# A decoder block on one core: all transposes of x put ahead of the modulation's rows, the rotary and lambda preparation moved into the first group, and the first weights loaded in four pieces

## The chip, the core and the metric

The kernel runs on one core of a Trainium2 chip. The metric is the device time of one execution in microseconds (us). A core has a matrix engine (TensorE, PE in the profile; its weight loads are PEld), a vector engine (VectorE, DVE), an activation engine (ScalarE, ACT), a general engine (GpSimd, POOL) and a queue engine that issues most transfers (SyncE, SP). Each engine takes its instructions in program order and waits for semaphores of the others.

## What is computed

One hybrid decoder block on x of 512 tokens by 1024 channels, float32. What matters here is its beginning:

```python
mod = (c @ w_ada[l] + b_ada[l])[:, None, :]
shift1, scale1, gate1, shift2, scale2, gate2 = jnp.split(mod, 6, axis=-1)
h = rmsnorm(x, norm1_w[l]) * (1.0 + scale1) + shift1
proj = h @ w_in[l]
...
qk = jax.nn.silu(causal_conv(jnp.concatenate([q_m, k_m], axis=-1), conv_w[l], conv_b[l]))
...
qd = partial_rope(rmsnorm(qd, q_norm_w[l]), positions)
kd = partial_rope(rmsnorm(kd, k_norm_w[l]), positions)
...
lam = (jnp.exp(jnp.sum(lam_q1[l] * lam_k1[l])) - jnp.exp(jnp.sum(lam_q2[l] * lam_k2[l])) + lam_init).astype(x.dtype)
```

After it come an mLSTM branch, a differential attention branch, an output projection and a mixture of 32 experts. The rotary tables (cos and sin of position times eight frequencies) and lambda are used only in the attention branch, long after the first projection.

## The kernel before, in words

The order of the instructions on each engine is the order in which the program text issues them; nothing reorders them later. Waits come from the tiles that instructions share and from the rings of buffers.

**Head.** SP loads x in four tiles of 128 tokens (L117), four lambda vectors of 64 numbers (L119), then through `load_ada0(fb)` (L142) the modulation weights of feature block fb, each block four transfers of 512 KB, with the first weights of `w_in` between them (`P0a`, units `wp`: one of 1024 KB and one loaded as two halves, L154 to L160). On POOL's own queue go the positions (L106) and, as broadcasts to all 128 partitions, the first 16 numbers of the q and k norm weights (`qkw16`, L109). SP waits at a transfer until the one eight places earlier has landed.

For each tile of x, ACT squares it and sums (L222), POOL makes the inverse root (L223, L193), DVE scales the tile (L225). `xT(j)` (L306) then transposes feature block j of all four tiles on PE (four transposes into one PSUM bank) and copies it back: even j on ACT (L315), odd j on DVE (L313). The banks are the four of ring `acc`, or for j of 4 and 5 the two of ring `t`.

`mod_rows(fb)` (L278) multiplies c with the modulation weights (16 matmuls on PE, L283) and ACT copies the row (L286); `mod_cols(fb)` (L288) turns the row into columns (8 small matmuls, L292) and DVE adds biases (L294 to L297) to the scale and shift `AB1`. `hT_pair(fb)` (L317) applies them to two blocks of x: the rounded part `hTh` on ACT (L324), the rest `hTl` on DVE (L325, L327). `warm(n)` issues n matmuls whose result nobody reads.

Between these calls of the head stand the angles (DVE L355 to L366, ACT Sin L368), lambda's products and Exp (L372 to L374, L384, L385), the rotary tables (eight DVE products, L382) and lambda's broadcast to the partitions (PE L394, DVE L395).

**First group.** `pstream` (L424) runs the projections as groups of eight chunks (a chunk is 128 rows of the contraction). `split` (L403) makes of a chunk's weights a rounded part `hi` on ACT (L407) and a rest `lo`, on POOL for one chunk and on DVE for the next (L408); it runs three chunks ahead. A chunk of the first group is 12 matmuls into four `acc` banks (L457 to L459). After chunk k, `hT_next(k)` (L329) adds the gate matmuls (L531, L532) and for k of 0, 2, 4 the next `mod_rows`, `mod_cols` and `hT_pair`. At a group's last chunk ACT copies out the four banks (L508, `craw`), and the next group's first chunk writes the same four banks. The convolutions of `ev_conv` (ACT L513, DVE L517, ACT Silu L524) follow through a list `later`; after each chunk `run` (L478) takes up to two of its entries, fewer when one answers "long". `param_cols` (L248: a small PE transpose and DVE steps L251 to L257) goes onto that list at k = 5 and so runs after chunk 5.

Of the kernel before, what the change touches and what calls it, by code (L numbers as in the profile page):

```python
# [33 lines left out]
R0, R1 = 3, 0  # L34
RT = (0, 0, 0, 0, 0)
REF = {4: 5, 7: 3, 11: 4}
W0 = (0, 2, 6)
EY, SY = 2, 0
W1 = 6
GF = False  # L40
# [17 lines left out]
def block_kernel(ctx, tc, x, c, positions, w_ada, b_ada, norm1_w, w_in, b_igate, b_fgate, conv_w, conv_b,  # L58
# [46 lines left out]
    mrow = dc.tile([24, 128], F32, name="mrow")  # L105
    G.dma_start(posi, positions[0].rearrange("(t p) -> t p", p=128))  # L106
    qkw16 = dc.tile([128, 2, 16], F32, name="qkw16")
    for i, w in enumerate((q_norm_w, k_norm_w)):
        G.dma_start(qkw16[:, i], bass.AP(tensor=w.tensor, offset=w.offset, ap=[[0, 128], [1, 16]]))  # L109
    cz = amc.rearrange("p a (k f) -> p (a k) f", f=32)  # L110
    S.dma_start(crow[0:8], c[0].rearrange("(j p) -> j p", p=128))
    S.dma_start(crow[8:16], norm1_w[0].rearrange("(j p) -> j p", p=128))
# [2 lines left out]
    xu = [U(f"x{a}", [128, 2, 1024]) for a in range(2)]  # L115
    for t in range(4):
        SP.dma_start(xu[t // 2][:, t % 2], x2[t * 128:(t + 1) * 128])  # L117
    for i, w in enumerate((lam_q1, lam_k1, lam_q2, lam_k2)):
        SP.dma_start(lamt[:, i], w)  # L119

    def ada_panel(ch, j):
        t = U("wada", [128, 2048])
# [19 lines left out]
    def load_ada0(fb):  # L142
        us = []
        for h in range(2):
            t = U("ada0", [128, 4, 2, 256])
            for s_ in range(2):
                SP.dma_start(t[:, :, s_], wada[h * 512:(h + 1) * 512, s_ * 1024 + fb * 256:s_ * 1024 + fb * 256 + 256]
                             .rearrange("(k p) f -> p k f", p=128))
            us.append(t)
        ada0[fb] = us  # L150

    P0a, P0b = [], []
    load_ada0(0)
    load_unit(P0a, 0, 0, 512)  # L154
    SP.dma_start(wif_raw, win[:, 2048:2056].rearrange("(k p) f -> p k f", p=128))
    load_ada0(1)
    P0a.append(U("wp", [128, 4, 512]))
    for i in range(2):
        SP.dma_start(P0a[1][:, 2 * i:2 * i + 2], win[512 + i * 256:768 + i * 256, 0:512].rearrange("(k p) f -> p k f", p=128))
        load_ada0(i + 2)  # L160
    SP.dma_start(rows[0:32], conv_w[0].rearrange("w (j p) -> (w j) p", p=128))
    SP.dma_start(rows[32:40], conv_b[0].rearrange("(j p) -> j p", p=128))
    SP.dma_start(rows[40:44], mlstm_norm_w[0])
# [165 lines left out]
    def hT_next(k):  # L329

        if GF:
            gates(k)
        if k in (0, 2, 4):
            fb = k // 2 + 1
            mod_rows(fb)
            if not GF:
                gates(k)
            mod_cols(fb)
            hT_pair(fb)
        elif not GF:  # L340
# [13 lines left out]
    for i in range(8):
        V.memset(invf[:, i:i + 1], INV_FREQ[i])  # L355
    xT(0)
    xT(1)
    V.tensor_mul(ang[:, 1], post[:, :, None].to_broadcast([128, 4, 8]), invf[:, None, :].to_broadcast([128, 4, 8]))
    V.tensor_scalar(kf, ang[:, 1], 1.0 / (2 * math.pi), MAGIC, op0=ALU.mult, op1=ALU.add)
    V.tensor_scalar(kf, kf, -MAGIC, None, op0=ALU.add)  # L360
    for cst in TWO_PI_PARTS:
        V.scalar_tensor_tensor(ang[:, 1], kf, -cst, ang[:, 1], op0=ALU.mult, op1=ALU.add)
    V.tensor_scalar(ang[:, 0], ang[:, 1], math.pi / 2, None, op0=ALU.add)
    V.tensor_scalar(kf, ang[:, 0], math.pi, -2 * math.pi, op0=ALU.is_gt, op1=ALU.mult)
    V.tensor_add(ang[:, 0], ang[:, 0], kf)
    V.tensor_scalar(ang, ang, -PI, PI, op0=ALU.max, op1=ALU.min)  # L366
    xT(2)
    S.activation(ang, ang, AF.Sin)  # L368
    xT(3)

    ls = dc.tile([1, 4], F32, name="ls")
    V.tensor_mul(lp, lamt[:, 0:4:2], lamt[:, 1:4:2])  # L372
    V.reduce_sum(ls[:, 0:2], lp, axis=AX.X)
    S.activation(ls[:, 0:2], ls[:, 0:2], AF.Exp)  # L374
    xT(4)
    xT(5)
    rope = []
    for i in range(2):
        tb = dc.tile([128, 4, 4, 8], F32, name=f"ropet{i}")

        for n, (cs, o_) in enumerate(((0, 0), (1, 8), (0, 8), (1, 0))):
            V.tensor_mul(tb[:, n], ang[:, cs], qkw16[:, i, None, o_:o_ + 8].to_broadcast([128, 4, 8]))  # L382
        rope.append(tb)
    V.tensor_sub(ls[:, 2:3], ls[:, 1:2], ls[:, 0:1])  # L384
    V.tensor_scalar(ls[:, 3:4], ls[:, 2:3], -(0.8 - 0.6 * math.exp(-0.3 * 0)), None, op0=ALU.add)  # L385
    warm(W0[0])
    mod_rows(0)
    xT(6)
    xT(7)
    warm(W0[1])  # L390
    mod_cols(0)
    nlam = const.tile([128, 1], F32, name="nlam")
    lamp = acc("lamp")
    PE.matmul(lamp[:, 0:1], ones[0:1, 0:1].to_broadcast([1, 128]), ls[:, 3:4], start=True, stop=True)  # L394
    V.tensor_copy(nlam, lamp[:, 0:1])  # L395
# [1133 lines left out]
```

## Time and profile before

| what | value |
|---|---|
| median of 3 runs | 716.75 us (714.95 to 717.03) |
| the profiled execution | 714.36 us, of which the span of instructions is 712.6 us |
| mean granted TensorE clock | 0.992 of full |
| PE busy | 669.8 us, 94% of the span |
| PEld, DVE, ACT, POOL busy | 69%, 53%, 33%, 28% |
| moved by DMA | 171.50 MB, mean 241 GB/s |

The rest, 1.76 us of the profiled execution, lies around the span. Times in the rows are us from the start of the span; where the rows merge several instructions, the count is behind "x" and the time is from the first one's start to the last one's end. The bracket at a row's end is the engine's idle time before it and what ended that.

### The profile page before, as it was taken

The page shows a single profiled execution, that of the slowest core. Times are in us where ns is not written, and L with a number is a line of the kernel's source. Part 1 is how long each engine was busy: PE and PEld are TensorE (multiplying, and loading weights), DVE is VectorE, ACT ScalarE, POOL GpSimd, SP SyncE. Part 2 cuts the span into 40 slices and gives each one's busy share as a digit, 9 for nine tenths or more (in the row PEclk, how much of TensorE's full clock was granted, in tenths as well). Part 3 has the DMA queues.
Part 4 walks back from the last instruction along what each step waited for, and adds up shares of the span by engine and source line. Part 5 has one row for each costly group of instructions (what it writes and reads, how often), then busy time and mean ns, then how long its engine had stood idle before and what let it go on. Part 6 is the DMA issues. An engine that isn't in the chain of part 4 may idle for free. (4 is left out here: it accounts for less than half of the span.)

```text
span 712.6 us, 11438 instructions
## 1 busy us (share of the span) xinstructions
PE 669.8 (94%) x4464; PEld 493.6 (69%) x4464; DVE 380.1 (53%) x765; ACT 236.1 (33%) x511; POOL 196.3 (28%) x204
## 2 busy tenths in 40 slices
PE   3999999999998999999999999699999999999972
PEld 2668887878777777778867888676667566766630
DVE  4746469866685467763795855763222332233211
ACT  5536582452443455542322234541111111111100
POOL 5213252436552213243253531121111121111100
PEclk9999999999999999999999999999999999999997
DMA  9973069215125011056636984779999999999971
GB/s 300 368 258 150 1 247 402 98 45 187 57 74 178 1 59 60 1 206 221 240 115 237 423 373 178 295 295 357 371 374 379 408 404 378 395 373 401 404 290 21
DMA packets 47386, 171.50 MB, mean 241 GB/s; under 512 B 8009, under 2 KB 16338, under 8 KB 32990
## 3 DMA queue, kind: packets, MB, share of 16 engines
q1 hardware_dynamic: 44510, 165.41, 60.2%
q0 software_dynamic: 2752, 5.28, 3.8%
q8 instruction: 37, 0.61, 0.3%
q14 instruction: 23, 0.19, 0.1%
q10 hardware_dynamic: 64, 0.02, 0.0%
HBM read 164.37 MB, written 10.51 MB: 245 GB/s over the span
## 5 line engine op out<-in xcount | busy, mean ns | idle before, releaser
L408 POOL TENSOR_TENSOR hl<-wp,hl 128x512 fp32r<-128x512 f32 x60 | 85.5, 1426 | 177.0 <-ACT hl L407 160.3
L407 ACT ACTIVATE hl<-wp 128x512 fp32r<-128x512 f32 x120 | 74.3, 627 | 104.0 <-PE acc L458 52.0
L1462 PE MATMUL gu<-we,he 128*64 128x256 f32 x784 | 93.2, 379 | 0.7 <-DMA we<-in_w_gate 0.7
L457 PE MATMUL acc<-hTh,hl 128*128 128x512 f32 x224 | 91.6, 409 | 0.3 <-ACT hTh L324 0.3
L458 PE MATMUL acc<-hTl,hl 128*128 128x512 f32 x224 | 88.4, 395 | 0.2 <-DVE hTl L327 0.2
L459 PE MATMUL acc<-hTh,hl 128*128 128x512 f32 x224 | 88.5, 395 | 0.0
L1462 PEld LDWEIGHTS gu<-we,he 128*64 128x64 f32 x784 | 59.6, 137 | 34.0 <-issue 6.8
L408 DVE TENSOR_TENSOR hl<-wp,hl 128x512 fp32r<-128x512 f32 x60 | 57.7, 963 | 46.8 <-ACT hl L407 46.8
L1308 PE MATMUL gp<-oh,xn 128*128 128x128 f16 x1024 | 64.0, 222 | 2.6 <-DVE oh L1296 1.7
L1308 PEld LDWEIGHTS <-xn 128*128 128x128 f16 x1024 | 60.2, 99 | 8.5 <-issue 5.4
L1469 ACT ACTIVATE sg<-gu 128x256 f32<-128x256 f32 x16 | 6.1, 383 | 173.5 <-PE gu L1462 173.5
L1493 POOL DMA_INDIRECT out<-y,ids x11 | 19.3, 1757 | 141.1 <-DVE y L1488 113.4
L1470 DVE TENSOR_TENSOR sg<-sg,gu 128x256 f32<-128x256 f32 x16 | 6.7, 421 | 94.4 <-ACT sg L1469 94.4
L457 PEld LDWEIGHTS acc<-hTh,hl 128*128 128x128 f32 x224 | 42.1, 188 | 15.4 <-issue 4.7
L461 PE MATMUL acc<-hl,hTh 128*128 128x512 f32 x128 | 52.5, 410 | 0.0
L463 PE MATMUL acc<-hl,hTl 128*128 128x512 f32 x128 | 50.2, 392 | 0.0
L462 PE MATMUL acc<-hl,hTh 128*128 128x512 f32 x128 | 50.1, 392 | 0.0
L1486 PE MATMUL o<-we,sg 128*64 128x512 f32 x192 | 48.3, 598 | 1.1 <-issue 1.1
L459 PEld LDWEIGHTS acc<-hTh,hl 128*128 128x128 f32 x224 | 42.2, 188 | 10.0
L458 PEld LDWEIGHTS acc<-hTl,hl 128*128 128x128 f32 x224 | 42.2, 188 | 9.1 <-DVE hTl L327 0.5
L826 DVE SCALAR_TENSOR_TENSOR wada<-wada,ccols 128x1024 f32<-128x1024 f32 x28 | 40.9, 1485 | 0.6 <-DMA wada<-in_w_ada 0.5
L1326 DVE TENSOR_SCALAR he<-gp,AB 128x128 f32<-128x128 f32 x64 | 21.9, 403 | 20.5 <-PE gp L1308 18.4
(353 smaller groups left out, 1148.9 us busy)
## 6 DMA issues: line engine op xcount, KB each, us to landing
we<-in_w_gate SPq DMA_DIRECT2D x25, 1024.0 KB
we<-in_w_up SPq DMA_DIRECT2D x24, 1024.0 KB
we<-in_w_down SPq DMA_DIRECT2D x24, 1024.0 KB
wp<-in_w_in SPq DMA_DIRECT2D x21, 1024.0 KB
wada<-in_w_ada SPq DMA_DIRECT2D x16, 1024.0 KB
ada<-in_w_ada SPq DMA_DIRECT2D x16, 512.0 KB
wx<-in_w_gate SPq DMA_DIRECT2D x6, 1024.0 KB
wp<-in_w_out SPq DMA_DIRECT2D x4, 1024.0 KB
```

The lines of the kernel that those rows point to most:

```text
L407: S.activation(hi, src, AF.Copy)
L408: (G if LP(n) else V).tensor_sub(lo, src, hi.bitcast(F32))
L457: PE.matmul(g.banks[b], wh[:, sl], ah, start=st, stop=False)
L458: PE.matmul(g.banks[b], wh[:, sl], al, start=False, stop=False)
L459: PE.matmul(g.banks[b], wl[:, sl], ah, start=False, stop=en)
L461: PE.matmul(g.banks[b], ah[:, sl], wh, start=st, stop=False)
L462: PE.matmul(g.banks[b], ah[:, sl], wl, start=False, stop=False)
L463: PE.matmul(g.banks[b], al[:, sl], wh, start=False, stop=en)
L826: V.scalar_tensor_tensor(t0[:, sl], cur[:, sl], ccol[:, j:j + 1], t0[:, sl], op0=ALU.mult, op1=ALU.add)
L1308: PE.matmul(ps_[c_][:, jj * 128:(jj + 1) * 128], part[t // 2][:, t % 2, c_ * 4 + jj], oh[i if st.get("first") else 2][:, t], start=first a ...
L1462: PE.matmul(gu[r, k * 256:(k + 1) * 256], h[:, j, r], wt[key, e][:, j], start=(j == 0), stop=(j == 7), skip_group_check=True)
L1486: PE.matmul(o[r], aT[:, j, r], wt["d", e][:, j, n * 512:(n + 1) * 512], start=(j == 0), stop=(j == 1), skip_group_check=True)
```

## The change

Four things are moved; the computation is the same.

1. All eight `xT(j)` stand ahead of `mod_rows(0)`; before, six did, and two stood behind it. `warm` is called with 0, 0 and 4 where it was 0, 2 and 6.
2. The frequencies, angles, Sin, lambda's products, Exp, rotary tables and lambda's broadcast become four functions `f0` to `f3`, put onto `later` behind `param_cols`: `param_cols` and `f0` run after chunk 5, `f1` and `f2` after chunk 6, `f3` and the first convolution after chunk 7. The broadcast's result sits in ring `t` instead of `acc`.
3. The two `qkw16` broadcasts are issued on POOL inside `f0`; the four lambda vectors are loaded by SP behind the row parameters of the first stage.
4. The first weights come as four pieces of 512 KB, each behind one block of modulation weights: block 0, piece 0, block 1, piece 1 and so on.

```diff
-W0 = (0, 2, 6)
+W0 = (0, 0, 4)
...
-    for i, w in enumerate((q_norm_w, k_norm_w)):
-        G.dma_start(qkw16[:, i], bass.AP(tensor=w.tensor, offset=w.offset, ap=[[0, 128], [1, 16]]))
...
-    for i, w in enumerate((lam_q1, lam_k1, lam_q2, lam_k2)):
-        SP.dma_start(lamt[:, i], w)
...
     load_ada0(0)
-    load_unit(P0a, 0, 0, 512)
-    SP.dma_start(wif_raw, win[:, 2048:2056].rearrange("(k p) f -> p k f", p=128))
-    load_ada0(1)
-    P0a.append(U("wp", [128, 4, 512]))
-    for i in range(2):
-        SP.dma_start(P0a[1][:, 2 * i:2 * i + 2], win[512 + i * 256:768 + i * 256, 0:512].rearrange("(k p) f -> p k f", p=128))
-        load_ada0(i + 2)
+    for i in range(4):
+        if i % 2 == 0:
+            P0a.append(U("wp", [128, 4, 512]))
+        SP.dma_start(P0a[i // 2][:, i % 2 * 2:i % 2 * 2 + 2],
+                     win[i * 256:i * 256 + 256, 0:512].rearrange("(k p) f -> p k f", p=128))
+        if i == 0:
+            SP.dma_start(wif_raw, win[:, 2048:2056].rearrange("(k p) f -> p k f", p=128))
+        if i < 3:
+            load_ada0(i + 1)
...
         elif k == 5:
             later.append(param_cols)
+            later.extend(angles())
...
+    def angles():
+        def f0():
+            for i, w in enumerate((q_norm_w, k_norm_w)):
+                G.dma_start(qkw16[:, i], bass.AP(tensor=w.tensor, offset=w.offset, ap=[[0, 128], [1, 16]]))
+            for i in range(8):
+                V.memset(invf[:, i:i + 1], INV_FREQ[i])
...
+        def f1():
...
+            V.tensor_scalar(ang, ang, -PI, PI, op0=ALU.max, op1=ALU.min)
+            S.activation(ang, ang, AF.Sin)
+            V.tensor_mul(lp, lamt[:, 0:4:2], lamt[:, 1:4:2])
+            V.reduce_sum(ls[:, 0:2], lp, axis=AX.X)
+            S.activation(ls[:, 0:2], ls[:, 0:2], AF.Exp)
+        def f2():
+            V.tensor_sub(ls[:, 2:3], ls[:, 1:2], ls[:, 0:1])
...
+        def f3():
...
+                    V.tensor_mul(tb[:, n], ang[:, cs], qkw16[:, i, None, o_:o_ + 8].to_broadcast([128, 4, 8]))
...
+            lamp = pt("lamp")
+            PE.matmul(lamp[:, 0:1], ones[0:1, 0:1].to_broadcast([1, 128]), ls[:, 3:4], start=True, stop=True)
+            V.tensor_copy(nlam, lamp[:, 0:1])
+        return [f0, f1, f2, f3]
+    for j in range(6):
+        xT(j)
     warm(W0[0])
+    for j in (6, 7):
+        xT(j)
     mod_rows(0)
-    xT(6)
-    xT(7)
     warm(W0[1])
     mod_cols(0)
```

On PE, between the transposes of blocks 4 and 5 and the first chunk, the order before was this (xtp are transposes, modp the modulation, lamp lambda's broadcast; two tiles of x, two transposes each, make a block):

```order
L283 MATMUL modp<-ada_99,amc 32x512 x4
L283 MATMUL modp<-ada_102,amc 32x512 x4
L309 MATMUL xtp<-ident,x_89 128x128 x2
L309 MATMUL xtp<-ident,x_90 128x128 x2
L309 MATMUL xtp<-ident,x_89 128x128 x2
L309 MATMUL xtp<-ident,x_90 128x128 x2
L276 MATMUL warm<-wi 64x512 x2
L292 MATMUL modp<-ones,ada_298 128x1 x4
L394 MATMUL lamp<-ls,ones 128x1
L276 MATMUL warm<-wi 64x512 x6
L457 MATMUL acc<-hTh_205,hl 128x512
```

and of the changed program at the same place:

```order
L311 MATMUL xtp<-ident,x_87 128x128 x2
L311 MATMUL xtp<-ident,x_88 128x128 x2
L285 MATMUL modp<-ada_93,amc 32x512 x4
L285 MATMUL modp<-ada_96,amc 32x512 x4
L294 MATMUL modp<-ones,ada_278 128x1 x4
L278 MATMUL warm<-wi 64x512 x4
L470 MATMUL acc<-hTh_204,hl 128x512
```

The last eight transposes went ahead of the modulation's rows; two of the warm matmuls in front of its columns, two behind them, and lambda's broadcast are gone from here.

On ACT, from the splits of chunks 8 and 9 (hl) on to the first group's copies (craw), the order before was this:

```order
L324 ACTIVATE hTh_206<-x_89,AB_204 128x256
L324 ACTIVATE hTh_206<-x_90,AB_204 128x256
L407 ACTIVATE hl<-wp 128x512 x3
L508 ACTIVATE craw<-acc 128x512 x4
L513 ACTIVATE cy<-craw,cols 128x512
```

and of the changed program:

```order
L420 ACTIVATE hl<-wp 128x512 x2
L379 ACT_TABLE_LOAD
L379 ACTIVATE ang<-ang 128x64
L383 ACT_TABLE_LOAD
L383 ACTIVATE ls<-ls 1x2
L420 ACTIVATE hl<-wp 128x512
L521 ACTIVATE craw<-acc 128x512 x4
```

Sin, Exp and a table load for each now stand between the split of chunk 9 and that of chunk 10, ahead of the four copies.

On DVE, behind `param_cols`, the changed program has the angles (f0, the split's lo of chunk 9, then f1), where before lo of chunk 9 came at once:

```order
L259 TENSOR_SCALAR qkcol<-qkcol 128x1
L366 MEMSET invf 128x1 x8
L367 TENSOR_TENSOR ang<-post,invf 128x32
L369 TENSOR_SCALAR kf<-ang 128x32
L370 TENSOR_SCALAR kf<-kf 128x32
L372 SCALAR_TENSOR_TENSOR ang<-kf,ang 128x32 x3
L421 TENSOR_TENSOR hl<-wp,hl 128x512
L375 TENSOR_SCALAR ang<-ang 128x32
L376 TENSOR_SCALAR kf<-ang 128x32
L377 TENSOR_TENSOR ang<-ang,kf 128x32
L378 TENSOR_SCALAR ang<-ang 128x64
```

All of these but the first and the split stood in the head before. Line numbers of the changed program are its own.

## Rows read from the trace of the kernel before

**Rows 1.** Whom PE waited for between 24 and 200 us: us in total, times, longest.
```profile
PE qkp L686 <- DVE E L615: 1.2, 2, 0.9
PE amp L568 <- DVE am L562: 0.6, 1, 0.6
PE acc L458 <- DVE hTl L327: 0.2, 1, 0.2
```

**Rows 2.** Timeline of PE in the head: start, us, instruction.
```profile
12.72 3.92 PE L309 MATMUL xtp<-ident,x 128*128 128x128 f32 x21 [1.48 <-DVE x L225]
16.58 1.92 PE L283 MATMUL modp<-ada,amc 128*32 128x512 f32 x16
...
20.32 0.95 PE L292 MATMUL modp<-ones,ada 128*128 128x1 f32 x8
...
23.42 0.51 PE L457 MATMUL acc<-hTh,hl 128*128 128x512 f32 x1 [0.32 <-ACT hTh L324]
```

**Rows 3.** Timeline of ACT in the head.
```profile
9.82 1.06 ACT L222 ACTIVATE junk<-x 128x1024 bf16<-128x1024 f32 x1 [1.41 <-DMA x<-in_x]
...
16.97 0.26 ACT L368 ACTIVATE ang<-ang 128x64 f32<-128x64 f32 x1
17.25 1.28 ACT L374 ACT_TABLE_LOAD   x1
18.54 0.20 ACT L374 ACTIVATE ls<-ls 1x2 f32<-1x2 f32 x1
...
19.18 0.57 ACT L286 ACTIVATE ada<-modp 128x512 f32<-128x512 f32 x1
...
22.27 2.08 ACT L324 ACTIVATE hTh<-x,AB 128x256 fp32r<-128x256 f32 x4 [1.48 <-DVE AB L297]
```

**Rows 4.** Timeline of DVE in the head.
```profile
9.96 0.75 DVE L225 TENSOR_SCALAR x<-x,ssq 128x1024 f32<-128x1024 f32 x1 [0.71 <-POOL ssq L193]
11.91 0.76 DVE L225 TENSOR_SCALAR x<-x,ssq 128x1024 f32<-128x1024 f32 x1 [1.20 <-POOL ssq L193]
...
14.76 0.18 DVE L358 TENSOR_TENSOR ang<-post,invf 128x32 f32<-128x32 f32 x1
...
16.74 0.20 DVE L366 TENSOR_SCALAR ang<-ang 128x64 f32<-128x64 f32 x1
...
21.57 0.60 DVE L297 TENSOR_TENSOR AB<-AB,ccols 128x2 f32<-128x2 f32 x1
```

**Rows 5.** One of the two broadcasts in the list of transfers (KB, and at the end us from issue to landing), and SP's issue of the first block of modulation weights, from the timeline.
```profile
qkw<-in_q_norm_w POOLq DMA_DIRECT2D x1, 8.0 KB, 6.8
...
6.17 4.00 SPq L147 DMA_DIRECT2D ada<-in_w_ada  x4
```

**Rows 6.** A stretch of 1 us: busy time of PE, PEld, DVE, ACT and POOL, then granted clock, DMA share and GB/s.
```profile
7.00:8.00 1.00, 0.19 (x2) 0.06 (x1) 0.81 (x4) 0.89 (x3) 0.68 (x2) 1.00 0.74 204
```

**Rows 7.** Stretches of 8 us, columns as in Rows 6.
```profile
0.00:8.00 8.00, 0.39 (x2) 0.29 (x2) 1.15 (x8) 4.33 (x6) 5.91 (x18) 1.00 0.78 244
8.00:16.00 8.00, 4.70 (x20) 3.83 (x21) 4.54 (x20) 3.25 (x9) 3.45 (x10) 1.00 1.04 351
16.00:24.00 8.00, 7.33 (x49) 4.13 (x47) 6.48 (x30) 6.42 (x14) 1.28 (x1) 1.00 1.10 357
24.00:32.00 8.00, 7.81 (x44) 4.90 (x45) 5.05 (x13) 3.60 (x9) 1.78 (x1) 1.00 1.08 372
```

**Rows 8.** Timeline of POOL: steps on x in the head, then lo of chunk 0 and of chunk 8.
```profile
8.54 0.75 POOL L223 TENSOR_SCALAR ssq<-ssq 128x1 f32<-128x1 f32 x1
9.38 0.55 POOL L193 TENSOR_TENSOR ssq<-ssq,mhalf 128x1 f32<-128x1 f32 x1
11.05 0.19 POOL L223 TENSOR_SCALAR ssq<-ssq 128x1 f32<-128x1 f32 x1 [1.13 <-ACT junk L222]
...
20.88 1.28 POOL L408 TENSOR_TENSOR hl<-wp,hl 128x512 fp32r<-128x512 f32 x1 [8.05 <-ACT hl L407]
...
53.34 1.74 POOL L408 TENSOR_TENSOR hl<-wp,hl 128x512 fp32r<-128x512 f32 x1 [8.03 <-ACT hl L407]
```

**Rows 9.** Stretches, counting the transposes of L309 alone: PE busy (x), PEld busy (x), granted clock, DMA share, GB/s.
```profile
13.00:15.00 2.00, 2.00 (x11) 2.00 (x11) 1.00 1.10 357
...
15.50:16.50 1.00, 1.00 (x10) 0.91 (x8) 1.00 1.04 385
```

**Rows 10.** Timeline, the second block of the modulation, inside the first group.
```profile
26.90 1.92 PE L283 MATMUL modp<-ada,amc 128*32 128x512 f32 x16
...
30.63 0.16 DVE L294 TENSOR_TENSOR AB<-modp,ccols 128x2 f32<-128x2 f32 x1 [2.60 <-PE modp L292]
```

**Rows 11.** Timeline of DVE at the end of the first group: lo of chunk 9, right behind `param_cols`, then the three steps of the first convolution.
```profile
55.55 0.69 DVE L408 TENSOR_TENSOR hl<-wp,hl 128x512 fp32r<-128x512 f32 x1
61.32 2.32 DVE L517 SCALAR_TENSOR_TENSOR cy<-craw,cols,cy 128x511 f32<-128x511 f32 x3 [5.08 <-ACT cy L513]
```

**Rows 12.** Timeline of ACT at the end of the first group: hi of chunk 10, then the four copies.
```profile
56.56 0.63 ACT L407 ACTIVATE hl<-wp 128x512 fp32r<-128x512 f32 x1 [2.78 <-PE acc L458]
57.89 2.69 ACT L508 ACTIVATE craw<-acc 128x512 f32<-128x512 f32 x4 [0.70 <-PE acc L459]
```

**Rows 13.** Timeline of PE: the first matmul of the second group on its first and on its second bank, two others between them.
```profile
60.25 0.39 PE L457 MATMUL acc<-hTh,hl 128*128 128x512 f32 x1
...
60.94 0.40 PE L457 MATMUL acc<-hTh,hl 128*128 128x512 f32 x1
```

More of the change, by code (lines that the diff above doesn't have):

```diff
@@ L167, in block_kernel @@
         SP.dma_start(rows[46:47, m * 64:(m + 1) * 64], k_norm_w)
+    for i, w in enumerate((lam_q1, lam_k1, lam_q2, lam_k2)):
+        SP.dma_start(lamt[:, i], w)
     gb = dc.tile([64, 1], F32, name="gb")
@@ L353, in block_kernel @@
     PI = 3.1415925
[L354 to L369, printed above, removed]
-    ls = dc.tile([1, 4], F32, name="ls")
-    V.tensor_mul(lp, lamt[:, 0:4:2], lamt[:, 1:4:2])
-    V.reduce_sum(ls[:, 0:2], lp, axis=AX.X)
-    S.activation(ls[:, 0:2], ls[:, 0:2], AF.Exp)
@@ L375, in block_kernel @@
-    xT(4)
-    xT(5)
-    rope = []
[L378 to L385, printed above, removed]
+    ls = dc.tile([1, 4], F32, name="ls")
@@ new lines, in block_kernel @@
+    nlam = const.tile([128, 1], F32, name="nlam")
+    rope = []
+    def angles():
[4 more added lines that the diff above has]
+                V.memset(invf[:, i:i + 1], INV_FREQ[i])
+            V.tensor_mul(ang[:, 1], post[:, :, None].to_broadcast([128, 4, 8]),
+                         invf[:, None, :].to_broadcast([128, 4, 8]))
+            V.tensor_scalar(kf, ang[:, 1], 1.0 / (2 * math.pi), MAGIC, op0=ALU.mult, op1=ALU.add)
+            V.tensor_scalar(kf, kf, -MAGIC, None, op0=ALU.add)
+            for cst in TWO_PI_PARTS:
+                V.scalar_tensor_tensor(ang[:, 1], kf, -cst, ang[:, 1], op0=ALU.mult, op1=ALU.add)
+        def f1():
+            V.tensor_scalar(ang[:, 0], ang[:, 1], math.pi / 2, None, op0=ALU.add)
+            V.tensor_scalar(kf, ang[:, 0], math.pi, -2 * math.pi, op0=ALU.is_gt, op1=ALU.mult)
+            V.tensor_add(ang[:, 0], ang[:, 0], kf)
+            V.tensor_scalar(ang, ang, -PI, PI, op0=ALU.max, op1=ALU.min)
[5 more added lines that the diff above has]
+            V.tensor_sub(ls[:, 2:3], ls[:, 1:2], ls[:, 0:1])
+            V.tensor_scalar(ls[:, 3:4], ls[:, 2:3], -(0.8 - 0.6 * math.exp(-0.3 * 0)), None, op0=ALU.add)
+        def f3():
+            for i in range(2):
+                tb = dc.tile([128, 4, 4, 8], F32, name=f"ropet{i}")
+                for n, (cs, o_) in enumerate(((0, 0), (1, 8), (0, 8), (1, 0))):
+                    V.tensor_mul(tb[:, n], ang[:, cs], qkw16[:, i, None, o_:o_ + 8].to_broadcast([128, 4, 8]))
+                rope.append(tb)
+            lamp = pt("lamp")
+            PE.matmul(lamp[:, 0:1], ones[0:1, 0:1].to_broadcast([1, 128]), ls[:, 3:4], start=True, stop=True)
+            V.tensor_copy(nlam, lamp[:, 0:1])
+        return [f0, f1, f2, f3]
@@ L386, in block_kernel @@
+    for j in range(6):
+        xT(j)
     warm(W0[0])
+    for j in (6, 7):
+        xT(j)
     mod_rows(0)
-    xT(6)
-    xT(7)
     warm(W0[1])
     mod_cols(0)
[L392 to L395, printed above, removed]
     warm(W0[2])
```

## The prediction

> **What bounds the kernel now.** I read whom PE waited for first, then the timelines of the head engine by engine, then the end of the first group, where the change puts what it takes out of the head. Between 24 and 200 us PE waited 2.0 us in all for other engines [rows 1]: once the first projection has begun, PE sets the pace and everything behind it slides with it. So two numbers matter: when the first chunk's matmul starts, 23.42 us now [rows 2], and whether a new hole opens in PE's work later. In the head the reader is to see one chain: the last tile of x lands, and ACT, free since 8.41, begins it at 9.82 after 1.41 us of waiting [rows 3]; POOL and DVE finish it at 12.67 [rows 4]; PE transposes from 12.72 [rows 2]; the modulation's rows run from 16.58; and the chain row, copy, columns, AB, hTh ends at 23.42.
>
> **The last tile of x.** The two qkw broadcasts are only 8 KB each but took up to 6.8 us to land, in the very time when x's tail is due [rows 5]; from 7 to 8 us the DMA engines were busy 0.74 of the time and moved 204 GB/s [rows 6], against 351 over the next eight [rows 7]. With the broadcasts gone, and the modulation weights issued behind x without the lambda vectors' detour (SP came to them at 6.17 only [rows 5]), I expect x's last tile by 8.4. ACT then begins it at 8.45 at best, its own limit, and its sum is there at about 9.7. That does not all come through. POOL is busy with the third tile until 9.93, and DVE scales the third tile from 9.96 to 10.71 [rows 4, 8]. POOL's first step on a tile took 0.75 us beside DVE's scaling and 0.19 alone [rows 8], so the fourth tile's ends at 10.72, its root 0.55 later at 11.3, DVE 0.76 later at 12.1, and PE starts at 12.15. Gain 0.57; bounds 0 (x is late for another reason) and 1.41 (the whole wait).
>
> **Transposes and modulation.** PE now has 29 transposes in a row, not 21. They come at 11 in 2 us until 15 us and at 10 in 1 us after 15.5 [rows 9]; the granted clock reads 1.00 throughout, but the pace doubles, as between the levels of 1.2 and 2.4 GHz, after PE had worked without a break from 12.72. I take 0.22 us each until 15.5 and 0.125 after (12.6 + 8.6, the 21 that ran). From 12.15: 15 slow ones to 15.5, 14 fast ones of 1.75 us, so the modulation's rows begin at about 17.25 instead of 16.58. Then the order pays. Before, the row's copy stood behind Exp on ACT and started at 19.18 [rows 3], and two warm matmuls stood ahead of the columns, which started at 20.32 [rows 2]. The second block shows the chain undisturbed: 3.73 us from its first matmul to AB's first step [rows 10]. By that AB begins at 17.25 + 3.73 = 20.98. It won't be shorter behind that: L297, with two inputs in SBUF, took 0.60 and ended with POOL's lo of chunk 0, at 22.16 [rows 4, 8], and lo will again be there: rows 1.92, copy 0.57, hi 0.6, lo 1.28 behind 17.25 make 21.7. L297 then ends at 21.8, and the first chunk's matmul comes 1.25 us later as it did now (22.17 to 23.42), at 23.05. Start gained: **0.4 us**, between 0 and 1.4.
>
> The removed warm matmuls and lambda's broadcast stood in waits of PE and cost nothing; should PE's idle time around the columns (two pieces of some 0.6 us) let the clock fall, the first chunk would show it.
>
> **The first weights.** Nothing is added in bytes. Ahead of the second piece, itself included, lie x with 2.1, two blocks with 4.2, two pieces with 1.05 MB and the small gate weights, 7.4 MB; the trace moved 7.6 MB by 24.0 [rows 7], so it lands at about 23.4. It holds chunk 2, and chunks take (60.25 - 23.42) / 8 = 4.6 us: PE wants it at about 32. The third piece ends at 10.0 MB, about 30.4 by the same rows, and is wanted from about 41. ACT, splitting ahead, may wait for them; PE has eight us of cover. Cost nothing. The lambda loads, behind the row parameters now, are wanted after 58 us: nothing.
>
> **What the angles do in the first group.** The angles are now on DVE behind `param_cols`, which ends at 55.55 or little later [rows 11], and the copies of the group's banks are queued on ACT behind Sin and Exp. In the clock of the trace before: memsets 0.2, f0's six steps and f1's four 2.18 together (14.76 to 16.94 [rows 4]), lo of chunk 9 between them 0.69 [rows 11], and 0.1 between: the angles are ready at 58.75. Sin's table is loaded by then, ACT being idle from 53.8 to 56.56 [rows 12]. From Sin's start to Exp's end took 1.77 us (16.97 to 18.74 [rows 3]), the table for Exp being loaded in between: 60.5. Then hi of chunk 10, 0.6: 61.1. The first copy, a quarter of 2.69 [rows 12]: 61.8. PE wants that bank at 60.25 [rows 13]; before, the copies began at 57.89 and were always ahead. **PE stands still for 1.55 us.** The next banks follow each 0.67 us, as fast as PE uses them (0.69 [rows 13]). Lambda's broadcast on PE needs Exp plus two small DVE steps, about 60.9, and lies within that hole. Bounds: 1.0 (DVE's steps run closer together) and 2.85 (another table load's 1.28 in the way). The rotary tables on DVE wait for the broadcasts: POOL is free for them at 55.1, behind lo of chunk 8 [rows 8], landing at about 62.3 by 6.8 us; DVE is held until 63.2, while ACT's copies last until 63.8 and the convolution comes behind them anyway. Nothing.
>
> Between Sin and Exp the table load took 1.28 us, and Exp started 0.01 us behind it [rows 3]. The Trainium skill's "ScalarE: Activation LUTs", section "What ACT_TABLE_LOAD costs", counts 1.28 us for the load and another 1.38 us of drain, 2.66 us for every switch; by it the hole would be 2.9 us and the sum 2.5. The trace before shows no such drain here, and the sum goes by the row.
>
> **Sum.** -0.4 + 1.55 = **+1.15 us**. Against the profiled execution: 714.36 + 1.15 = 715.5. The median of the runs shown, 716.75, is 2.4 above that execution, and executions of the kernel differ by 2.7 us; I put the forecast on the median: 717.9.
>
> **The rivals.**
> - *No hole* (the copies come in time, or PE has slack I don't see): only the start remains, 716.75 - 0.4 = 716.3, at best 715.3. For it: DVE idles 5.08 us ahead of its convolutions [rows 11], so the angles have room. Against: ACT is in order, and Sin can't come before 58.7.
> - *Not what it says* (x's last tile lands at 9.8 still, because the modulation weights now follow at once): PE starts at 12.72; the eight transposes ahead cost 1.0, the shorter chain gives back 1.05, so nothing is gained: +1.55, 718.3.
> - *Slower, by the table switch*: if ACT pays a second 1.28 between Sin and Exp, the hole is 2.85 and the sum +2.45, 719.2. It decides once Exp ends so late that hi and the first copy (1.3) end behind 60.25, from 58.95 on. Against it stands Exp 0.01 us behind its load. The drain of the Trainium skill's "ScalarE: Activation LUTs" would be this case.
> - *Slower, by the broadcasts' landing*: DVE in order holds behind the tables three convolution steps (2.32 [rows 11]) and lo of chunk 11 (0.69), wanted on PE three chunks of 12 matmuls, 8.3 us, behind 61.8, at 70.1. Back from there, with the tables' own 1.0, they may start at 66.0: up to 10.9 us from POOL's readiness cost nothing, each us beyond is paid by PE. At twice the landing of before (69.3) that is +3.3, with the sum 721.2. Against: 6.8 was measured in dense traffic.
>
> **How the numbers follow.** Forecast 0.50, no hole 0.21, not what it says 0.14, table switch 0.09, landing 0.06. A measurement of this kernel can tell about 0.3%, 2.15 us, from no change. The forecast lies within it, with some of its spread above; so do the first two rivals, of which the first reaches below only at its best end together with the runs' scatter; the last two lie mostly above. That makes faster 0.07, same 0.73, slower 0.20. The range goes from the best end of "no hole" less a us of scatter, 714.3, to the table switch plus the same, 720.2, and leaves out the landing and little more.
>
> **What would show it.** ACT's fourth square at about 8.5 without a long wait; PE's transposes as one block of 29 from about 12.1; the modulation's rows at 17.2 and the first chunk at 23.0. About 60 us: Sin near 58.4, Exp at 60, copies from about 60.7, and a wait of PE of some 1.5 us for ACT's copies, where there was none. I am wrong if PE's wait there is under 0.5 or over 2.5 us, if the first chunk starts before 22 or after 23.5, or if a difference of over a microsecond appears behind 75 us, for which nothing in this working gives a reason.

## The result: slower by 0.5%

The changed kernel took 719.25 us (median of 7 runs, 718.13 to 719.60) against 715.62 us of the kernel before on the same chip (7 runs, 713.25 to 717.03): a ratio of 1.0052 with a 95% interval of 1.0036 to 1.0067. Forecast were 717.9 us and no change that can be told. The time lies inside the stated range, 714.3 to 720.2, but not in the likeliest case's place: the kernel became slower, which had been given 0.20.

The profiled execution took 718.57 us with a span of 716.9 us and a mean granted clock of 0.985; before it was 714.36, 712.6 and 0.992. The execution is 4.2 us longer, and landmarks on PE show where it grew:

| PE begins, us from the span's start | before | after | difference |
|---|---|---|---|
| transposes of x's last tile | 12.72 | 12.17 | -0.55 |
| the modulation's rows | 16.58 | 17.23 | +0.65 |
| the first chunk | 23.42 | 22.96 | -0.46 |
| the second block of the modulation, behind chunk 0 | 26.90 | 28.68 | +1.78 |
| the second group | 60.25 | 63.52 | +3.27 |
| the third group | 104.70 | 108.03 | +3.33 |

Up to the first chunk the change gains, as forecast. Then it loses 2.24 us within a single chunk, where nothing had been forecast, and 1.49 us more up to the second group. Between the second and the third group nothing is added. Behind that the execution is 0.9 us longer still.

### The profile after, in the head

PE's timeline, the rows that answer to [rows 2], with the second block of [rows 10] as the last:

```profile
12.17 5.12 PE L311 MATMUL xtp<-ident,x 128*128 128x128 f32 x29 [1.00 <-DVE x L227]
17.23 1.92 PE L285 MATMUL modp<-ada,amc 128*32 128x512 f32 x16
19.87 1.05 PE L294 MATMUL modp<-ones,ada 128*128 128x1 f32 x8 [0.72 <-ACT ada L288]
20.78 1.11 PE L278 MATMUL warm<-wi 128*64 128x512 f32 x4
22.96 0.80 PE L470 MATMUL acc<-hTh,hl 128*128 128x512 f32 x1 [1.06 <-ACT hTh L326]
23.68 0.80 PE L471 MATMUL acc<-hTl,hl 128*128 128x512 f32 x1
24.28 0.63 PE L472 MATMUL acc<-hTh,hl 128*128 128x512 f32 x1
...
28.68 2.27 PE L285 MATMUL modp<-ada,amc 128*32 128x512 f32 x16
```

The block of 29 transposes, the rows at 17.23 and the chunk at 22.96 stand where the prediction put them. New are two pieces of idle time, 0.72 and 1.06 us, with 128x1 matmuls and four warm ones between them, and the length of a matmul of the first chunk: 0.80, where it was 0.51 [rows 2]. The stretches say why. PE's busy time (x instructions), then granted clock, DMA share and GB/s, first of after:

```profile
22.00:23.00 1.00, 0.04 (x1) 0.80 1.04 378
23.00:24.00 1.00, 1.00 (x2) 0.50 1.10 356
24.00:26.00 2.00, 2.00 (x6) 0.50 1.11 349
26.00:28.00 2.00, 2.00 (x6) 0.50 1.10 348
28.00:30.00 2.00, 2.00 (x14) 0.64 1.08 375
```

and of the kernel before:

```profile
22.00:23.00 1.00, 1.00 (x5) 1.00 1.10 375
23.00:24.00 1.00, 0.61 (x2) 1.00 1.07 366
24.00:26.00 2.00, 1.86 (x8) 1.00 1.08 368
```

After, PE is busy for 0.04 us between 22 and 23, and within that microsecond the granted clock leaves 1.00. It reads 0.50, the lower of TensorE's two levels (1.2 and 2.4 GHz), until behind 29 us, while PE works without a break, six matmuls in 2 us. Before, there are eight in that time and the clock stays at 1.00. From the first chunk to the second block took 5.72 us instead of 3.48; with the second block, begun at half clock (2.27 us instead of 1.92), about 2.6 us went here.

ACT's third and fourth square of x, to set beside [rows 3]:

```profile
7.65 1.06 ACT L224 ACTIVATE junk<-x 128x1024 bf16<-128x1024 f32 x1 [0.56 <-DMA x<-in_x]
8.98 1.06 ACT L224 ACTIVATE junk<-x 128x1024 bf16<-128x1024 f32 x1 [0.17 <-DMA x<-in_x]
```

The fourth comes at 8.98 instead of 9.82 and waits 0.17 us for x instead of 1.41.

### The profile after, at the end of the first group

ACT, answering to [rows 12]:

```profile
55.92 1.28 ACT L379 ACT_TABLE_LOAD   x1
60.70 0.26 ACT L379 ACTIVATE ang<-ang 128x64 f32<-128x64 f32 x1 [3.49 <-DVE ang L378]
60.97 1.28 ACT L383 ACT_TABLE_LOAD   x1
62.27 0.20 ACT L383 ACTIVATE ls<-ls 1x2 f32<-1x2 f32 x1
62.38 0.61 ACT L420 ACTIVATE hl<-wp 128x512 fp32r<-128x512 f32 x1
62.89 2.00 ACT L521 ACTIVATE craw<-acc 128x512 f32<-128x512 f32 x4
```

and PE, answering to [rows 13]:

```profile
62.14 0.39 PE L545 MATMUL pif<-hTl,wi 128*128 128x512 f32 x1
62.97 0.35 PE L397 MATMUL lamp<-ls,ones 1*128 1x1 f32 x2 [0.44 <-DVE ls L387]
63.52 0.50 PE L470 MATMUL acc<-hTh,hl 128*128 128x512 f32 x1 [0.20 <-ACT craw L521]
```

Sin waits 3.49 us for DVE's angles, its table loaded long before. Exp follows its own load by 0.02 us, then come hi of chunk 10 and the four copies, and PE, through with the gate matmuls 0.23 us (their distance) behind 62.14, begins the second group at 63.52 instead of 62.37: a hole of 1.15 us with lambda's broadcast in it.

### The profile page after: what moved, and what is told of

It reads as the page before. It is cut to its first block, busy times and chain, and to the rows that moved or that the text cites. A ratio compares the mean times of both kernels' runs of the same rounds, so it can differ in the third digit from the quotient of the medians.

```text
span 716.9 us, 11434 instructions
## 1 busy us (share of the span) xinstructions
PE 673.5 (94%) x4460; PEld 495.9 (69%) x4460; DVE 380.8 (53%) x765; ACT 235.8 (33%) x511; POOL 197.7 (28%) x204
## 5 line engine op out<-in xcount | busy, mean ns | idle before, releaser
L470 PE MATMUL acc<-hTh,hl 128*128 128x512 f32 x224 | 92.7, 414 | 1.3 <-ACT hTh L326 1.1
L472 PE MATMUL acc<-hTh,hl 128*128 128x512 f32 x224 | 89.5, 399 | 0.0
L1321 PE MATMUL gp<-oh,xn 128*128 128x128 f16 x1024 | 65.5, 225 | 1.7 <-DVE oh L1309 1.7
```

The lines of the kernel that those rows point to most:

```text
L470: PE.matmul(g.banks[b], wh[:, sl], ah, start=st, stop=False)
L472: PE.matmul(g.banks[b], wl[:, sl], ah, start=False, stop=en)
L1321: PE.matmul(ps_[c_][:, jj * 128:(jj + 1) * 128], part[t // 2][:, t % 2, c_ * 4 + jj], oh[i if st.get("first") else 2][:, t], start=first a ...
```

## Experiments

The theory behind the first four: the idle time around the columns, which the four removed warm matmuls (two ahead of the columns, two behind) had filled, drops the clock and costs 2.6 us; the angles cost 1.1. Rivals: the order of the transposes itself, lambda's loads, the weight pieces. A last rival is chance: that the clock falls in some executions whatever stands there. Ratios are to the kernel before on the same chip, with 95% intervals; the medians come from several chips (1 to 4, 5 to 8 and 9 to 11 share one each), so kernels of different chips are compared by their ratios.

| kernel | median us | ratio | fourth square | transposes | first chunk | chunk 0 | 2nd group |
|---|---|---|---|---|---|---|---|
| before | | | 9.82 | 12.72 | 23.42 | 3.48 | 60.25 |
| after | 719.25 | 1.0052 (1.0036 to 1.0067) | 8.98 | 12.17 | 22.96 | 5.72 | 63.52 |
| 1 after, 8 warm | 716.02 | 1.0013 (0.9999 to 1.0027) | 8.93 | 12.18 | 23.06 | 3.49 | 61.03 |
| 2 after, old head | 715.45 | 1.0004 (0.9992 to 1.0016) | 9.39 | 12.43 | 23.24 | 3.49 | 61.20 |
| 3 before, 4 warm | 716.44 | 1.0024 (1.0010 to 1.0038) | 10.79 | 13.69 | 24.70 | 4.87 | 62.90 |
| 4 before, new head | 717.10 | 1.0015 (0.9999 to 1.0030) | 10.59 | 13.82 | 24.52 | 5.71 | 63.74 |
| 5 as 1, broadcasts back | 717.81 | 1.0029 (1.0014 to 1.0045) | 10.42 | 13.33 | 24.16 | 3.48 | 62.00 |
| 6 after, late angles | 716.79 | 1.0018 (1.0003 to 1.0032) | 9.15 | 12.21 | 22.68 | 5.72 | 61.94 |
| 7 as 6, 8 warm | 714.45 | 0.9992 (0.9978 to 1.0006) | 8.96 | 12.22 | 22.82 | 3.49 | 59.62 |
| 8 before, four pieces | 716.16 | 1.0007 (0.9987 to 1.0027) | 9.41 | 12.35 | 23.24 | 3.48 | 60.04 |
| 9 as 6, old head | 714.19 | 0.9990 (0.9978 to 1.0002) | 9.15 | 12.20 | 23.18 | 3.48 | 59.98 |
| 10 after, 6 warm | 716.27 | 1.0010 (0.9991 to 1.0028) | 8.76 | 12.16 | 24.13 | 3.49 | 62.08 |
| 11 as 1, lambda back | 715.45 | 1.0006 (0.9989 to 1.0022) | 8.61 | 12.07 | 23.67 | 3.48 | 61.65 |
| 12 before, 2 and 8 warm | 714.80 | 0.998 (0.996 to 1.000) | 9.67 | 12.61 | 23.54 | 3.49 | 60.38 |

The middle columns are starts in one profiled execution each, in us: ACT's fourth square, PE's transposes of the last tile and the first chunk; "chunk 0" is the time from the first chunk to the second block of the modulation. It sorts the kernels: in all four profiles with four warm matmuls the clock fell there, and in none of the ten with six or more. That speaks against chance.

**1. Eight warm matmuls instead of four, all else as changed.**

```diff
-W0 = (0, 0, 4)
+W0 = (0, 0, 8)
```

> The changed kernel with eight warm matmuls instead of four between the modulation's columns and the first chunk, nothing else. Theory idle (PE's idle time before the first chunk let the clock fall at 22.6 us, and that is the largest part of the loss): PE has work until about 22.9, the clock of the first chunk stays at 2.4 GHz, the second block of the modulation starts near 26.5 instead of 28.68, and the time falls by about 2.5 us, from 719.25 to 716.7. Rival chance (the clock falls in some executions whatever stands there): half clock at 22.6 again, 719.2. Rival hole (the wait at the end of the first group is the loss, the clock only looks bad): 719.0.

```profile
20.88 2.04 PE L278 MATMUL warm<-wi 128*64 128x512 f32 x8
23.06 0.50 PE L470 MATMUL acc<-hTh,hl 128*128 128x512 f32 x1
26.55 1.92 PE L285 MATMUL modp<-ada,amc 128*32 128x512 f32 x16
...
61.03 0.50 PE L470 MATMUL acc<-hTh,hl 128*128 128x512 f32 x1 [0.20 <-ACT craw L521]
```

On PE's timeline no idle time of note stands ahead of the first chunk, which comes 0.10 us later than after and takes 3.49 us; the second group begins 2.49 us earlier. The 0.72 us ahead of the columns are still there and do no harm by themselves. Four matmuls that nobody reads are worth 0.39% (1.0052 to 1.0013, intervals apart).

**2. The old head in the changed kernel**: the order of the transposes and the warm matmuls of before, the rest as changed.

```diff
-W0 = (0, 0, 4)
+W0 = (0, 2, 6)
...
+    mod_rows(0)
     for j in (6, 7):
         xT(j)
-    mod_rows(0)
```

> The changed kernel with PE's head as before: transposes of blocks 6 and 7 behind the modulation's rows, warm matmuls 0, 2 and 6; angles, broadcasts and weights stay where the change put them. Theory idle: clock stays full, first chunk at about 22.6 to 22.9 (x still lands early), the hole of about 1.1 us at the end of the first group is still there, so 715.6 - 0.6 + 1.1 = 716.1. Rival chance: as the changed kernel, 719. Rival hole: 718.5 to 719, since the hole is untouched.

The clock holds here too. From the last tile's transposes to the first chunk it took 10.81 us with the old order, and 10.88 with the new one in experiment 1. These are single profiles: over all of them the stretch takes 10.70 to 11.01 us with the old order and 10.47 to 11.97 with the new one, so some tenths could hide here. The ratios of 7 and 9 below, 0.9992 and 0.9990, show no difference either.

**3 and 4. From the other side, in the kernel before**: its warm matmuls cut as the change does, then the new order as well.

```diff
-W0 = (0, 2, 6)
+W0 = (0, 0, 4)
```

> The kernel before with warm matmuls 0, 0 and 4 instead of 0, 2 and 6, nothing else. Theory idle, if the warm matmuls alone held the clock: half clock in the first chunk, 715.6 + 2.5 = 718.1. Theory idle, if the transposes behind the rows suffice: clock stays, 715.6 or up to 0.5 less, as the columns come 0.5 us earlier. Rival chance: 715.6.

Experiment 4 has the same line and this:

```diff
-    mod_rows(0)
     xT(6)
     xT(7)
+    mod_rows(0)
```

> The kernel before with part 1 of the change alone: all transposes ahead of the modulation's rows and warm matmuls 0, 0 and 4; angles, broadcasts and loads stay in the head. Theory idle: PE idles around the columns as in the changed kernel, half clock in the first chunk, and no hole at the end of the first group: 715.6 + 2.5 to 3.0 = 718.1 to 718.6. Rival chance: 715.6. Rival hole: 715.6, since the hole isn't there.

PE in experiment 3:

```profile
22.31 1.14 PE L276 MATMUL warm<-wi 128*64 128x512 f32 x4
24.70 0.49 PE L457 MATMUL acc<-hTh,hl 128*128 128x512 f32 x1 [1.25 <-ACT hTh L324]
...
26.44 0.63 PE L457 MATMUL acc<-hTh,hl 128*128 128x512 f32 x1
...
29.57 1.92 PE L283 MATMUL modp<-ada,amc 128*32 128x512 f32 x16
```

Two of its stretches (PE's busy time, granted clock, DMA share, GB/s):

```profile
25.00:26.00 1.00, 0.77 (x2) 0.53 1.05 372
...
28.00:30.00 2.00, 2.00 (x10) 0.88 1.12 377
```

PE in experiment 4, and the stretch in which its clock fell:

```profile
21.43 1.05 PE L292 MATMUL modp<-ones,ada 128*128 128x1 f32 x8 [0.85 <-ACT ada L286]
...
22.72 1.14 PE L276 MATMUL warm<-wi 128*64 128x512 f32 x4
24.52 0.79 PE L457 MATMUL acc<-hTh,hl 128*128 128x512 f32 x1 [0.66 <-ACT hTh L324]
```

```profile
23.00:24.00 1.00, 0.86 (x4) 0.91 1.10 377
```

The clock fell in both profiles. In 3 it fell only inside chunk 0 (a matmul takes 0.49 us at 24.70, 0.63 at 26.44) and, by these stretches, was back at full 3.4 us later, where it took 6.8 us in the changed kernel; so less was lost there, 1.39 us. In 4 the whole chunk ran at half speed, as after. There the clock fell at about 23.8, when the four warm matmuls were just ending and the idle time ahead of the chunk had not begun; what stood before it were 0.85 us of idle time ahead of the columns. So the idle piece right before the chunk is not needed for the fall. In time both stayed below what was expected: 3 took 716.44 and 4 took 717.10, where 718.1 and 718.1 to 718.6 had been put down. The ratio of 4 is +0.15%, its median against the kernel before on that chip (717.10 to 715.29) +0.25%, and the profile's 2.23 us would be 0.3%. The runs of 4 lie between 715.18 and 719.06 with the profiled one at the top; whether the clock fell in each of them isn't known.

**5. The broadcasts back in the head** of the changed kernel with eight warm matmuls.

```diff
-W0 = (0, 0, 4)
+W0 = (0, 0, 8)
...
+    for i, w in enumerate((q_norm_w, k_norm_w)):
+        G.dma_start(qkw16[:, i], bass.AP(tensor=w.tensor, offset=w.offset, ap=[[0, 128], [1, 16]]))
...
-            for i, w in enumerate((q_norm_w, k_norm_w)):
-                G.dma_start(qkw16[:, i], bass.AP(tensor=w.tensor, offset=w.offset, ap=[[0, 128], [1, 16]]))
```

> The changed kernel with eight warm matmuls (so that the first chunk's clock stays full), and with the two qkw broadcasts back in the head on POOL; lambda's loads stay where the change put them. Theory broadcasts (they held up x's last tile): ACT's fourth square waits again for x, past 9.8 us instead of 8.98, PE's last transposes begin at 12.7 to 13.8 instead of 12.18, the first chunk at 23.6 to 24.6 instead of 23.06; 716.0 + 0.5 to 1.5 = 716.5 to 717.5. Rival lambda (the four lambda loads and their waits on SP held x up): start as with the broadcasts away, 12.2 and 23.1, 716.0.

ACT in experiment 5, the last two squares:

```profile
8.78 1.06 ACT L226 ACTIVATE junk<-x 128x1024 bf16<-128x1024 f32 x1 [1.88 <-DMA x<-in_x]
10.42 1.06 ACT L226 ACTIVATE junk<-x 128x1024 bf16<-128x1024 f32 x1 [0.49 <-DMA x<-in_x]
```

With two transfers of 8 KB alone put back, x's last square went from 8.93 (experiment 1) to 10.42. Over all profiles the fourth square stands at 9.41 to 10.79 with them in the head and at 8.61 to 9.39 without: on average 1.1 us apart, though the ends nearly touch. The ratio went from 1.0013 to 1.0029, but the two intervals overlap, so that it costs time in the end is not shown.

**6 and 7. The angles one group later**, with four and with eight warm matmuls. They are given to chunks 0, 4, 5 and 6 of the second group, whose copies come later.

```diff
-            later.extend(angles())
...
-        def f0():
+        def fq():
             for i, w in enumerate((q_norm_w, k_norm_w)):
...
+
+        def f0():
...
+    for k, f in zip((0, 4, 4, 5, 6), angles()):
+        at(1, k, f)
```

Experiment 7 also has `W0 = (0, 0, 8)`.

> The changed kernel with the angles and lambda one group later (broadcasts after chunk 8, f0 and f1 after chunk 12, f2 after 13, f3 after 14) and four warm matmuls as in the change. Theory idle: the clock still falls in the first chunk; without the hole of 1.1 us the second group starts at about 62.4 instead of 63.52; 719.25 - 1.1 = 718.1. Rival hole: back to 716 or less. If Sin and Exp there stand in front of something else, PE shows a new wait near 77 to 83 us.

> Both mends together: the changed kernel with eight warm matmuls and the angles one group later. Theory idle: first chunk at 23.05 at full clock, second group at about 59.9 instead of 61.03 with eight warm matmuls alone; 716.0 - 1.1 = 714.9, against 715.3 for the kernel before. Rival chance: nothing, 716 to 719.

ACT and PE in experiment 7 at the end of the first group:

```profile
55.93 0.63 ACT L421 ACTIVATE hl<-wp 128x512 fp32r<-128x512 f32 x1 [2.77 <-PE acc L472]
57.27 2.70 ACT L522 ACTIVATE craw<-acc 128x512 f32<-128x512 f32 x4 [0.70 <-PE acc L473]
```

```profile
59.62 0.39 PE L471 MATMUL acc<-hTh,hl 128*128 128x512 f32 x1
```

ACT now waits for PE, the copies begin 2.35 us before PE wants the first bank back, and PE passes into the second group without a hole. From the second block of the modulation to the second group took 33.31 us in 7, against 34.48 in 1: the hole is 1.17 us. Between 6 and 7, which differ by four warm matmuls alone, lie 2.32 us at the second group and 2.34 us in the medians: the price of the clock a second time. So the angles, which cost 1.2 us at the end of the first group, make PE wait for nothing in the second. Lambda's broadcast now stands among its matmuls there:

```profile
79.27 0.38 PE L398 MATMUL lamp<-ls,ones 1*128 1x1 f32 x2
```

The second group takes 44.9 to 45.0 us in the three kernels with late angles (6, 7 and 9) and 44.4 to 44.6 in all others, so some 0.4 us of the 1.2 come back as cost, about what the broadcast takes. The ratios show more than these landmarks: late angles bring 0.34% with four warm matmuls (after to 6) and 0.21% with eight (1 to 7), 2.4 and 1.5 us. Experiment 6 was expected at 718.1 and took 716.79; what it gained beyond the hole stays open.

**8. Only the four weight pieces**, in the kernel before: the `load_unit` and the loop of two replaced by the loop of four as in the change's diff.

> The kernel before with part 4 of the change alone, the first weights in four pieces. As predicted it costs and brings nothing: 715.3, no wait of PE in the first group. If the second or third piece is late, a wait of PE or of ACT for wp appears between 24 and 42 us and the time is up to 1 us longer.

No effect that can be told; the second group begins at 60.04, before at 60.25.

**9. As 6, with the old head of experiment 2.** It keeps the change's loads and lets go of the order.

> The changed kernel with PE's head as before (transposes of blocks 6 and 7 behind the modulation's rows, warm matmuls 0, 2 and 6) and the angles one group later. Theory order-is-neutral (the place of the last eight transposes moves the first chunk by under 0.2 us, and matters only through the clock): as with eight warm matmuls and late angles, 714.5, second group at about 60.0, full clock in the head. Rival order-pays (all transposes first brings something by itself): 0.5 us or more above that, 715.

PE in experiment 9:

```profile
23.18 0.51 PE L471 MATMUL acc<-hTh,hl 128*128 128x512 f32 x1 [0.72 <-ACT hTh L326]
```

By the ratios it takes 0.6% less than the changed kernel, with intervals well apart. Against the kernel before its interval just takes in 1. In this profile 0.72 us of idle time ahead of the first chunk left the clock at full: the matmul takes 0.51.

**10. Six warm matmuls** in the changed kernel.

```diff
-W0 = (0, 0, 4)
+W0 = (0, 0, 6)
```

> The changed kernel with six warm matmuls instead of four. PE then works until about 22.3 and idles some 0.5 us before the first chunk, instead of 1.06 with four and almost nothing with eight. Theory idle leaves open where the clock turns: if it holds, the second modulation block starts 3.5 us behind the first chunk and the time is 716.0; if it falls, 5.7 us behind and 718.5 to 719.2.

```profile
21.95 1.58 PE L278 MATMUL warm<-wi 128*64 128x512 f32 x6
24.13 0.50 PE L470 MATMUL acc<-hTh,hl 128*128 128x512 f32 x1 [0.60 <-ACT hTh L326]
27.62 1.92 PE L285 MATMUL modp<-ada,amc 128*32 128x512 f32 x16
```

Six hold the clock over 0.60 us of idle time ahead of the chunk; four with 1.06 (after) or 0.66 (experiment 4) did not. The chunk is late here because the transposes stayed slow until about 18.2 us in this execution.

**11. Lambda's loads back in the head** of the changed kernel with eight warm matmuls.

```diff
-W0 = (0, 0, 4)
+W0 = (0, 0, 8)
...
+    for i, w in enumerate((lam_q1, lam_k1, lam_q2, lam_k2)):
+        SP.dma_start(lamt[:, i], w)
...
-    for i, w in enumerate((lam_q1, lam_k1, lam_q2, lam_k2)):
-        SP.dma_start(lamt[:, i], w)
```

> The changed kernel with eight warm matmuls and the four lambda loads back in SP's head, between x and the modulation weights; the broadcasts stay in the first group. Theory broadcasts: x's last tile still arrives at about 9.0 and the first chunk stands at 23.1; the modulation weights are issued 3.5 us later but are there by 17; 716.0. Rival lambda: fourth square past 9.8 us and 716.5 to 717.5.

x's last square comes at 8.61, no later than without them. So lambda's loads are not what holds x up, which leaves the broadcasts.

**12. Eight warm matmuls behind the columns, instead of six, in the kernel before.** Its 94 timed runs up to then had a mean granted clock of 0.9866, the one profile 0.992, so it might itself lose the clock at times.

```diff
-W0 = (0, 2, 6)
+W0 = (0, 2, 8)
```

> The kernel before with eight warm matmuls instead of six between the columns and the first chunk. The mean granted clock of the runs so far: 0.9866 over 94 runs of the kernel before (0.982 to 0.991; the profiled execution 0.992), 0.984 to 0.985 for the kernels whose profile shows a chunk at half clock, 0.989 to 0.991 for those with six or eight warm matmuls behind the new head. Theory: the kernel before itself loses the clock ahead of its first chunk in a part of its executions; then the mean clock here is about 0.989 and the median about 1 us lower, a ratio of 0.998 to 0.999. Rival: its mean clock is lower for a stretch elsewhere; then the mean clock stays at 0.987 and the ratio is 1.000 to 1.0005, the start being up to 0.2 us later for the longer block of warm matmuls.

Inconclusive. The ratio, 0.998 with an interval of 0.996 to 1.000, is the theory's; the mean clock, 0.987 over 12 runs, is the rival's, and in its own profile the clock is at full in the head and low elsewhere (0.90 between 450 and 500 us). There it is low in every profile, 0.90 to 0.97, and in 4 and 12 it fell once more between 200 and 250 us; so the mean clock of a run does not tell whether the head lost it.

## Why the prediction was right in its range, and which of its steps failed

**The number: luck in part.** The change was forecast at +1.15 us and measured at +3.63 in the medians. The time still lies inside the range for two reasons that have nothing to do with the working. The forecast stood on a median of three runs of the kernel before, 716.75, and over seven it is 715.62; and the upper part of the range was made for a second table load, which did not come. Put on 715.62, the range would have ended at about 719.1, just below the measured time. None of the prediction's three signs of being wrong came up either, since none of them looked at how fast the first chunk runs.

**The start: right.** Forecast were -0.4 us and a first chunk at 23.05; measured -0.46 and 22.96. Tile, rows and AB were forecast at 12.15, 17.25 and 20.98 and came at 12.17, 17.23 and 20.96. One step is off without consequence: ACT's fourth square came at 8.98, not 8.45, because the third tile was late too (ACT waited 0.56 us for it). POOL was through with the third tile by then and waited 0.36 us for ACT, but its step took 0.48 us, not 0.19, and ended with DVE's scaling of the third tile (10.69 against 10.64), so that DVE set the end, as argued:

```profile
10.21 0.48 POOL L225 TENSOR_SCALAR ssq<-ssq 128x1 f32<-128x1 f32 x1 [0.36 <-ACT junk L224]
```

```profile
9.89 0.75 DVE L227 TENSOR_SCALAR x<-x,ssq 128x1024 f32<-128x1024 f32 x1 [0.71 <-POOL ssq L195]
```

That the broadcasts held x up was argued there from their landing times; the fourth square in experiment 5 bears it out. That the first chunk came so near to its forecast is luck in part: with the same order of the head but more warm matmuls it began at 22.82 (7) to 24.13 (10), by when the transposes changed their pace.

**The order of the transposes: no difference shown, as forecast.** Eight more ahead (+1.20 us from the last tile's transposes to the rows) and a shorter chain behind (6.84 to 5.73 us from the rows to the first chunk) cancel between before and after; experiments 1 and 2 differ by 0.07 us over both. The 6.84 belong to the one profile of before: the five other profiles with the old order show 6.34 to 6.37, so the shorter chain is worth less than the 1.05 us that the prediction counted.

**The warm matmuls: wrong, and this is the step that failed.** The prediction put down that they "cost nothing", named the clock as a condition in the same sentence, and carried no term, no rival and no chance for it. It looked at the idle time of PE only as time for others to finish in. Their worth lay in what came next: with four instead of eight around the columns the clock fell to 0.50 between 22 and 23 us and the first chunk paid. That the number of warm matmuls decides is shown by the experiments; that it does so through the idle time they fill is argued. The missing term was worth about 2.6 us by the landmarks, 2.34 by the medians of 6 and 7, 0.39% by after against experiment 1. With that term the sum would have been 3.5 to 3.75 us, against 3.63 measured in the medians. The first chunk did show it, as the prediction said, but in its length, 5.72 us instead of 3.48; the prediction had given bounds for its start alone, and the chunk began on time.

**The hole: the mechanism right, the size too large.** Forecast 1.55 us, bounds 1.0 to 2.85; measured 1.15. Two parts of it came out smaller. The angles came at 60.67, 1.70 us before PE wanted its bank (62.37), against 1.50 forecast: DVE's steps ran closer together, 2.93 us from `param_cols` to the last one's end instead of 3.2, as its timeline shows (first and last row). And the price of a copy, a quarter of the 2.69 us of [rows 12], was too high, since that row holds waits between the copies; four of them in a row took 2.00. The two differences, 0.20 and 0.17, make the 0.4.

```profile
57.59 0.15 DVE L259 TENSOR_SCALAR qkcol<-qkcol 128x1 f32<-128x1 f32 x1
...
60.47 0.20 DVE L378 TENSOR_SCALAR ang<-ang 128x64 f32<-128x64 f32 x1
```

**The rivals.** No hole: fell, it is there. Not what it says: fell, x's last tile came earlier. The table switch: fell, Exp starts 0.02 us behind a load of 1.28. The Trainium skill's "ScalarE: Activation LUTs", section "What ACT_TABLE_LOAD costs", adds a drain of 1.38 us to each switch; here none stands between the load and Exp, nor between Sin's end and the load (0.01 us), so the measurement decides against it for this place. The broadcasts' landing: fell. (Its times were added up to 0.6 us too late: 6.8 us behind 55.1 is 61.9 and not 62.3, twice that 68.7 and not 69.3, and its price 2.7 us and not 3.3; the forecast does not use them.) One landed within 4.8 us, less than the 6.8 of [rows 5]:

```profile
qkw<-in_q_norm_w POOLq DMA_DIRECT2D x1, 8.0 KB, 4.8
```

**The weight pieces: right**, by experiment 8 and by PE's waits after, from 15 to 100 us (total, times, longest), of which none is for a weight; the first two are the idle pieces of the head and the last two belong to the hole:

```profile
PE acc L470 <- ACT hTh L326: 1.1, 1, 1.1
PE modp L294 <- ACT ada L288: 0.7, 1, 0.7
PE lamp L397 <- DVE ls L387: 0.4, 1, 0.4
PE acc L470 <- ACT craw L521: 0.2, 1, 0.2
```

**Open.** The 0.9 us behind the third group. From there to the end the profiles of all kernels took 606.5 to 609.5 us with no order by what was changed, so it may be scatter. Open too is what the kernel before loses of the clock in its ordinary runs (experiment 12), and why the change of pace of the transposes, at 15.2 to 18.2 us over the profiles, moves: it shifts the start by up to a microsecond, whatever the kernel.

## What to carry to other kernels

Matmuls that nobody reads, ahead of a dense stretch, were priced here by the stretch behind them: before removing some, look at the granted clock of that stretch, even when they only filled waits. Work moved out of a crowded head wants a place where the engine in order has nothing due behind it; here the second group had it and the first group's last chunks did not. Small broadcasts issued beside a load that the start waits for are worth trying to move: of the four parts of this change it is the only one whose gain shows, in the start and not clearly in the whole time.

## What the runs showed of the hardware

The clock fell for little: idle pieces of 0.72 and 1.06 us with small work between them, ahead of a full load, brought 6.8 us at half clock (about 22.6 to 29.4). In experiment 4 it fell after 0.85 us of idle time and in 3 after 1.25; 0.72 and 0.14 us (1), 0.72 and 0.60 (10), or 0.72 ahead of the chunk alone (2 and 9) did not bring it. No length of idle time parts the two sets, so what number of such matmuls is enough can be told for this head only. The fall can also come inside the dense work, as in experiment 3: a first matmul at 0.49 us says nothing of the tenth. The Trainium skill's "TensorE: Matmul & The Clock Gate", section "A second HAM failure mode: psum-queue depth-cycling", tells of a kernel where PE idling briefly and often between groups of matmuls made the clock go up and down; this trace shows a single fall behind two brief idle pieces, worth 2.6 us, and no going up and down.

Two broadcasts of 8 KB to 128 partitions, on another queue than x, went with a later end of a load of 2.1 MB: by 1.5 us between two profiles (8.93 to 10.42), by 1.1 us on average over all of them.
